# Where the last quarter of layer 0's gate projection runs, and where the last head group's prompt unit stands

## The chip, the core and the metric

The kernel runs on one core of one Trainium2 chip. A core has a matrix engine (TensorE, PE in the profile; its weight loads are shown as PEld), a vector engine (VectorE, DVE), an engine for activation functions (ScalarE, ACT), a general one (GpSimd, POOL) and a queue engine that issues transfers (SyncE, SP). The engines run at the same time, each through its own list of instructions in order, and wait for each other by semaphores. The metric is the time of one execution on the device, in microseconds (us); smaller is better. Of the kernel before, three runs took 864.18, 865.16 and 865.75 us, median 865.16.

## The reference, cut to what matters

One step of a two-layer network on 640 tokens: 512 latent ones ("sample") and 128 context ones ("prompt"), 1024 features each. Layer 0 is grouped-query attention with a gate, layer 1 a gated linear recurrence. The change is in layer 0, which per token stream computes:

```
shift, scale, gate = split(silu(cond) @ ada_w + ada_b)
h   = x * (1 + scale) + shift
q, k, v, g = split(h @ w_in)            # 1024, 256, 256, 1024 columns
q, k = rms_norm(q), rms_norm(k)         # with rotary positions on latent tokens
o   = softmax(q @ k.T / 8) @ v          # 16 query heads on 4 key heads of 64
out = (o * silu(g)) @ w_out
x   = layer_norm(alpha * x + gate * out)
```

Prompt tokens attend to prompt tokens only; sample tokens attend to 128 cached positions and all 512 sample tokens (640 keys). The part that the change moves is the last quarter of `silu(g)`: 256 of the 1024 gate columns, which are multiplied into the outputs of the last four query heads.

## The kernel before, in words

**Precision.** Matrices are kept as a high and a low part in a rounded fp32 format (`hi` and `lo`); a product takes three matmuls: hi by hi, hi by lo, lo by hi. The modulated input `h` is held feature by token in `hhi` and `hlo`, eight blocks (`KT`) of 128 features by 640 tokens. A weight arrives from memory as `raw` pieces of 512 KB; `split_piece` (line 217) casts the piece to `hi` on ScalarE and subtracts on VectorE for `lo`.

**The stream of raw pieces.** `order` (lines 357 to 374) lists all weight pieces in the order in which they are used, and `pump` (line 193) issues their transfers from SP's queue in this order, two ahead, into a ring of three buffers. So a piece cannot be issued before the one ahead of it in the list. `attn_w_in` is cut in chunks of 256 columns, two pieces each: chunks 0 to 3 are q, one per head group, and 6 to 9 are the gate. `ada_pieces(sup)` are eight pieces of the modulation's weights.

**Lead-in.** After keys and values, `lead_in` (line 658) computes q of head group 0 and then the gate: chunks 6 to 9, for each chunk two column blocks of 128 (`mt`) by two token halves of 320 (`j`), which is sixteen units. A unit is `feat_mms` (line 324), 24 matmuls into one PSUM bank, and a Silu on ScalarE into `gs` (line 746); `gs` has eight blocks of 128 columns by 640 tokens, and chunk `ch` and `mt` fill block `2 * (ch - 6) + mt`. Between the units stand the jobs that normalise, rotate, split and transpose q and k (`later`, with `settle` for the transposes). In the last `EARLY` = 2 units, attention is started by `next(att)`.

**Attention.** `att_gen` (line 885) runs over 36 units: for each of four head groups `c`, a `prompt_unit` and then eight `sample_unit`s (a head and a half of the sample queries each). A unit has fronts (scores, maximum, Exp with a sum; the reciprocal and the scaling on GpSimd follow), backs (transposes of the probabilities, copied out of PSUM) and an end. Fronts run two units ahead. Two neighbouring sample units share an end: `apply`, twenty TensorE instructions in the profile into `pot`, and `av_out` (line 786), which multiplies `gs` in place. `pot` and the prompt's `potp` share a pool with one buffer (`pop`). Blocks `2c` and `2c + 1` of `gs` belong to group `c`, and the prompt's `av_out` touches the last 128 tokens of both.

**PSUM.** In this phase there are two double banks (`bank2`, the scores), three single banks (`bank1`: q projection and transposes, ada, transposes of probabilities) and the one of `pop`. Each set is a ring that is handed out in the order in which the program is written.

**Side work.** `weave` (line 84) drives attention and, 0.62 times per step (`SIDE_B`), one step of a list called `side`, strictly in the list's order: `q1`, `q2`, `q3` (the q projections of groups 1 to 3, each with eight ada pieces), then `a` (the last ada), `w` (`prefetch_gen`: the first four pieces of the output projection's weights, in the room that the in-projection's weights leave) and `s` (`split_gs` of blocks 0 to 5). `split_gs` casts finished blocks of `gs` into `hhi` and subtracts into `hlo`, whose old contents, the modulated input, must no longer be needed. An item may have a condition: `q` of group `c` starts when fronts have come to group `c - 1`, `a` when a unit of group 3 has ended. `side.until(name)` forces a list item to its end at that point.

**The end of layer 0.** Blocks 6 and 7 are split last (line 1119), then come the other weight pieces, and from line 1260 on the output projection, token block by token block.

**Order.** All this lies in one block (`first_half`, lines 165 to 1121) whose instructions a planner lays out anew on each engine when the kernel is built; it may put an instruction that is ready ahead of one that was written earlier. Only what is marked `keep_in_program_order` stays in place. The program's order thus sets priorities and the rings of buffers, not the exact order on an engine.

Of the kernel before, what the change touches and what calls it, by code (L numbers as in the profile page):

```python
# [38 lines left out]
EARLY = 2  # L39
# [91 lines left out]
def hybrid_step(ctx: ExitStack, tc: tile.TileContext, a: dict, o: dict):  # L131
# [177 lines left out]
    def ada_gen(sups):  # L309
        for sup in sups:  # L310
            acc = rowp.tile([P, CW], F32, tag="row", name="acc")
            nc.gpsimd.dma_start(acc, a["ada_bias"][sup])
            for i in range(4):
                ps = bank1("adaps")
                ada_mms(ps, sup, i)
                nc.vector.tensor_tensor(acc, acc, ps[:, :CW], ALU.add)
                yield
            yield
            ada_out(sup, acc)
            yield  # L320
            if sup == 0:
                gate_load(0, nc.gpsimd)

    def feat_mms(ps, w, mt, j, hhi, hlo):
        c, t = slice(mt * P, (mt + 1) * P), slice(*HALVES[j])
        for k in range(KT):
            nc.tensor.matmul(ps[:, :320], w.hi(k)[:, c], hhi[:, k, t], start=(k == 0), stop=False)  # L327
            nc.tensor.matmul(ps[:, :320], w.hi(k)[:, c], hlo[:, k, t], start=False, stop=False)  # L328
            nc.tensor.matmul(ps[:, :320], w.lo(k)[:, c], hhi[:, k, t], start=False, stop=(k == KT - 1))  # L329

    def tok_gen(out, w, tt, hhi, hlo):
        t = slice(tt * P, (tt + 1) * P)
# [21 lines left out]
    def ada_pieces(sup):  # L354
        return [("ada_s", sup, k) for k in range(KT)]
# [7 lines left out]
        if c4 == 1:  # L363
            order.append(("rope",))
    FIRST = set(order)
    for c in (0, 6, 7, 8, 9):
        order.extend(pieces("attn_w_in", c))
    for c in range(3):
        order.extend(pieces("attn_w_in", c + 1))
        order.extend(ada_pieces(c))  # L370
    order.extend(ada_pieces(3))
    order.extend(("attn_w_out", nh, i) for nh, i in PIECES)
    order.extend(("rec_w_in", h, i) for h in range(RH) for i in range(5))
# [284 lines left out]
    def lead_in(att):  # L658
        backs = deque()
        ws = {0: first_w}  # L660

        def settle():
            while backs:
                backs.popleft()()

        rk = rtab.tile([P, NKV * TT], F32, name="rk")

        def k_stats():
            ss = rtab.tile([P, NKV * TT], F32, name="ssk")
            for tt0, m in UNITS:  # L670
                t = kr[tt0] = rtab.tile([P, m * CW], F32, tag=f"kr{tt0}", name="kr")
                for i in range(m):
                    nc.scalar.activation(t[:, i * CW:(i + 1) * CW], acc[tt0 + i][:, :CW], AF.Square)
                nc.vector.tensor_reduce(ss[:, NKV * tt0:NKV * (tt0 + m)], t[:].rearrange("p (h d) -> p h d", d=HD), AX.X, ALU.add)
            rsqrt(rk, ss, 1.0 / HD, NORM_EPS)

        def k_norm():
            for tt0, m in UNITS:
                for i in range(m):
                    tt = tt0 + i  # L680
                    nc.vector.tensor_tensor(view(kr[tt0], i * CW, [[HD, NKV], [1, HD]]),
                                            acc[tt][:, :CW].rearrange("p (h d) -> p h d", d=HD),
                                            view(rk, NKV * tt, [[1, NKV], [0, HD]]), ALU.mult)

        def k_rope(n):
            tt0, m = UNITS[n]
            rope_apply(kr[tt0], tt0, m, cosk, sink, kg, kr[tt0])
            if tt0 == TS:
                nc.gpsimd.dma_start(o["new_k"], kr[tt0])

        def k_split(n):
            tt0, m = UNITS[n]
            backs.append(split_k(kr[tt0], m, P * (tt0 + 1)))

        def v_job(tt):
            (nc.scalar.copy, nc.vector.tensor_copy)[tt % 2](vv[:, tt + 1, :], acc[tt][:, CW:])
            if tt == TS:
                nc.gpsimd.dma_start(o["new_v"], vv[:, tt + 1, :])

        rq = rtab.tile([P, NKV * TT], F32, name="rq")  # L700

        def q_stats():
            ss = rtab.tile([P, NKV * TT], F32, name="ssq")
            for n, (tt0, m) in enumerate(UNITS):
                squares(q0[n], m, ss[:, NKV * tt0:NKV * (tt0 + m)])
            rsqrt(rq, ss, 1.0 / HD, NORM_EPS)

        def q_job(n):
            tt0, m = UNITS[n]
            r = rope_apply(rms_apply(q0[n], m, rq, NKV * tt0), tt0, m, cosq, sinq, qg)  # L710
            back = q_split(r, tt0, m, 0, Xs[0], bank_any)
            backs.append(lambda: [back(i) for i in range(m)])

        ck = prep.tile([P, CW], F32, tag="ck", name="ck")
        tc.keep_in_program_order(nc.scalar.dma_start(ck, a["cache_k"]))
        tc.keep_in_program_order(nc.scalar.dma_start(vv[:, 0, :], a["cache_v"]))
        ws[6] = Weights("attn_w_in", 6, LEAD_LO)
        w = ws.pop(0)
        q0, kr = [], {}
        for n, (tt0, m) in enumerate(UNITS):  # L720
            ps = bank_any("pmm")
            for i in range(m):
                drain(tok_gen(ps[:, i * CW:(i + 1) * CW], w, tt0 + i, hhi, hlo))
            q0.append(ps)
            if n == 0:
                k_stats()
                for tt in range(TT):
                    v_job(tt)
                k_norm()
            else:  # L730
                k_rope(n - 1)
        open_rest()
        q_stats()
        k_rope(2)
        later = [lambda n=n: q_job(n) for n in range(3)] + [lambda: backs.append(split_k(ck, 1, 0))]
        later += [lambda n=n: k_split(n) for n in range(3)]
        step = 0
        for ch in range(6, 10):
            if ch < 9:
                ws[ch + 1] = Weights("attn_w_in", ch + 1, LEAD_LO)  # L740
            w = ws.pop(ch)
            for mt in range(2):
                for j, (t0, t1) in enumerate(HALVES):
                    ps = bank_any("gps")
                    feat_mms(ps, w, mt, j, hhi, hlo)
                    nc.scalar.activation(gs[:, 2 * (ch - 6) + mt, t0:t1], ps[:, :320], AF.Silu)
                    step += 1
                    if step % 2 or not later:
                        settle()
                    if step % 2 and later:  # L750
                        later.pop(0)()
                    if step > 16 - EARLY:
                        next(att)


# [129 lines left out]
    def att_gen(side):  # L885
        units = []
        for c in range(4):
            units.append(prompt_unit(c))
            units += [sample_unit(c, 2 * pr + j, qh) for pr in range(2) for qh in range(2) for j in range(2)]
        AHEAD = 2  # L890

        def fronts(u):
            if u >= len(units):
                return []
            c, fr = units[u][:2]
            front_of[0] = c
            side.until(f"q{c}")
            return list(fr)

        def run(f):  # L900
            f()
            tick()

        for u in range(AHEAD):
            for f in fronts(u):
                run(f)
                yield
        pending = []

        def flush():  # L910
            while pending:
                run(pending.pop(0))
                yield

        for u, (c, _, back, end) in enumerate(units):
            fr = fronts(u + AHEAD)
            for n, b in enumerate(back):
                run(b)
                yield
                if n == 1:  # L920
                    yield from flush()
                if n and fr:
                    run(fr.pop(0))
                    yield
            for f in fr:
                run(f)
                yield
            back_of[0] = c
            if end:
                pending.append(end if len(back) == 2 else end())  # L930
        yield from flush()
        while later:
            tick()
# [59 lines left out]
    def prefetch_gen():  # L993
# [2 lines left out]
        woa.append(ws.enter_context(pool("woa", 1)))  # L996
        yield from wo_gen(0, PIECES[:4], woa[0])

    def q_next(c):
        Xs[c] = xq[c % 2].tile([P, 4, NT], F32R, tag="X", name=f"X{c}")  # L1000
        yield from q_gen(c, Xs[c], ada_gen((c - 1,)))

    for c in range(1, 4):
        side.items.append((f"q{c}", q_next(c), lambda c=c: front_of[0] >= c - 1))
    side.items.append(("a", ada_gen((3,)), lambda: back_of[0] == 3))
    side.items += [("w", prefetch_gen()), ("s", split_gs(range(6)), lambda: back_of[0] == 3)]
    weave(att, side, SIDE_B)
# [634 lines left out]
```

## Time and profile before

The profile shows one execution, which took 863.82 us.

| quantity | value |
|---|---|
| median of three runs | 865.16 us |
| profiled execution | 863.82 us |
| its span, first to last instruction | 862.1 us |
| around the span | 1.7 us |
| instructions | 19366 |
| mean granted TensorE clock | 0.986 |
| moved by transfers | 92.50 MB |

The span falls into these stages: start, modulation, keys and values up to some 62 us; q of group 0 up to 73; the sixteen gate units from 72.9 to 135.6; attention with q projections beside it up to 281.7, where the last q matmul starts; the last head group up to 343.8; then the output projection and layer 1.

How to read the lines: a row of the view by stretch gives the stretch and its length, the busy time of each engine with its number of instructions, the granted TensorE clock (1.00 is full), the transfers' share and rate. A row of the timeline gives start, length, engine, line, operation, output and inputs with shapes and count; in square brackets the engine's idle time before it and what ended that. A row of the view of waits gives who waited for whom, total us, times, the longest. A row of groups ends with count, busy us, mean ns and the idle time before. The lines of the kernel are meant by L and a number.

### The profile page before, as it was taken

Reading aid. Unit: us, or ns where it says so; the run is one execution under the profiler, and the core shown is the slowest. Engines: PE = TensorE matmul, PEld = TensorE weight load, DVE = VectorE, ACT = ScalarE, POOL = GpSimd, SP = SyncE. Lnnn points to the kernel's source line nnn. Section 1 sums busy time; section 2 is a strip of 40 time slices with the busy share of each in tenths; the row PEclk is TensorE's granted clock in tenths of the full one; section 3 lists DMA queues with packets and bytes.
Section 4 is the critical chain, followed back from the end, with each engine's and each line's share of the span. In section 5 each row is a group of like instructions: output and inputs, shape, how many; then the busy total and the mean of one; then the engine's idle time right before and its main releaser. Section 6 shows DMA issues by size and latency. Waiting matters only on the chain.

```text
span 862.1 us, 19366 instructions
## 1 busy us (share of the span) xinstructions
PE 818.7 (95%) x8144; PEld 734.0 (85%) x8144; DVE 530.9 (62%) x952; ACT 384.0 (45%) x767; POOL 211.8 (25%) x263
## 2 busy tenths in 40 slices
PE   6999999989999998999999999999999999999993
PEld 4789998768778756888899999999999999897783
DVE  3556435755746656776437575757667576858384
ACT  2232536554655766232434544444444345443240
POOL 0123002434434652010001314142333233110101
PEclk9999999999999999999999999999999999999996
DMA  9932212143242162621223322332413323242221
GB/s 339 364 98 86 84 40 75 50 172 130 86 141 75 49 205 90 233 109 59 80 68 71 103 64 81 81 112 69 111 57 93 93 82 98 75 149 68 66 112 73
DMA packets 33990, 92.50 MB, mean 107 GB/s; under 512 B 5024, under 2 KB 12208, under 8 KB 33904
## 3 DMA queue, kind: packets, MB, share of 16 engines
q1 hardware_dynamic: 22992, 72.95, 25.0%
q0 software_dynamic: 4864, 14.44, 5.5%
q10 hardware_dynamic: 6048, 3.88, 1.5%
q8 instruction: 64, 1.05, 0.5%
q14 instruction: 22, 0.18, 0.1%
HBM read 82.06 MB, written 9.19 MB: 106 GB/s over the span
## 4 chain that ended last, share of the span: by engine, by line
PE 85%; DVE 6%; ACT 3%; DMA 2%; issue 2%; POOL 1%; ACTq 0%; DVEq 0%; POOLq 0%
PE rps L1192 7%; PE rps L1193 6%; PE rps L1194 6%; PE vgps L1182 4%; PE vgps L1184 4%; PE vgps L1183 4%; PE outp L1031 4%; PE pot L784 4%; PE outp L1032 4%; PE outp L1033 4%; PE pt L866 3%; PE lv L1324 2%; PE gps L327 2%; PE gps L328 2%; PE gps L329 2%; PE sc L757 2%
## 5 line engine op out<-in xcount | busy, mean ns | idle before, releaser
L1192 PE MATMUL rps<-h1hi,rhi 128*128 128x320 f32 x368 | 118.3, 321 | 0.0
L1193 PE MATMUL rps<-h1lo,rhi 128*128 128x320 f32 x368 | 113.7, 309 | 0.0
L1194 PE MATMUL rps<-h1hi,rlo 128*128 128x320 f32 x368 | 113.6, 309 | 0.0
L859 POOL TENSOR_SCALAR p<-p,rc 128x640 f32<-128x640 f32 x64 | 54.6, 856 | 69.2 <-DVE rc L858 53.0
L1192 PEld LDWEIGHTS rps<-h1hi,rhi 128*128 128x128 f32 x368 | 69.2, 188 | 1.3
L1193 PEld LDWEIGHTS rps<-h1lo,rhi 128*128 128x128 f32 x368 | 69.2, 188 | 0.0
L1194 PEld LDWEIGHTS rps<-h1hi,rlo 128*128 128x128 f32 x368 | 69.1, 188 | 0.0
L222 DVE TENSOR_TENSOR rlo<-raw,rhi 128x1024 fp32r<-128x1024 f32 x32 | 45.4, 1421 | 33.9 <-ACT rhi L221 33.9
L854 ACT ACTIVATE p<-sc,nm 128x640 f32<-128x640 f32 x64 | 51.2, 801 | 28.8 <-DVE nm L851 22.1
L1352 POOL COPY At<-near 32x160 f32<-32x160 f32 x32 | 14.0, 438 | 196.2 <-DVE near L1314 195.2
L851 DVE TENSOR_REDUCE nm<-sc 128x1 f32<-128x640 f32 x64 | 52.0, 819 | 15.5 <-PE sc L758 15.3
L1302 ACT COPY kc<-A 128x640 f32<-128x640 f32 x40 | 32.3, 807 | 59.4 <-DVE A L1333 51.7
L221 ACT CAST rhi<-raw 128x1024 fp32r<-128x1024 f32 x32 | 33.6, 1049 | 52.0 <-PE rps L1193 48.4
L866 PE MATMUL pt<-small,p 128*128 128x128 f32 x320 | 50.5, 279 | 2.5 <-ACT pts L762 1.3
L1182 PE MATMUL vgps<-rhi,h1hi 128*128 128x256 f32 x180 | 51.7, 287 | 1.2 <-ACT h1hi L982 1.2
L1184 PE MATMUL vgps<-rhi,h1lo 128*128 128x256 f32 x180 | 51.0, 283 | 0.4 <-DVE h1lo L983 0.4
L1183 PE MATMUL vgps<-rlo,h1hi 128*128 128x256 f32 x180 | 50.9, 283 | 0.0
L762 ACT COPY pts<-pt 128x512 f32<-128x512 f32 x64 | 36.3, 590 | 29.4 <-PE pt L866 29.2
L866 PEld LDWEIGHTS pt<-small,p 128*128 128x128 f32 x320 | 37.4, 141 | 11.3 <-issue 7.4
L757 PE MATMUL sc<-kk,X 128*128 128x320 f32 x128 | 43.0, 344 | 2.9 <-ACT p L854 2.7
L1182 PE MATMUL vgps<-wspare,h1hi 128*128 128x256 f32 x140 | 41.7, 298 | 0.0
L327 PE MATMUL gps<-hhi,whi 128*128 128x320 f32 x128 | 40.0, 312 | 0.4 <-ACT X L610 0.4
(291 smaller groups left out, 2393.5 us busy)
## 6 DMA issues: line engine op xcount, KB each, us to landing
raw<-in_rec_w_in SPq DMA_DIRECT2D x40, 512.0 KB, 3.6
raw<-in_ada_s SPq DMA_DIRECT2D x32, 512.0 KB, 3.6
raw<-in_ada_m SPq DMA_DIRECT2D x16, 512.0 KB, 8.4
raw<-in_attn_w_in SPq DMA_DIRECT2D x16, 512.0 KB, 4.2
raw<-in_attn_w_out SPq DMA_DIRECT2D x8, 512.0 KB, 4.0
raw<-in_rec_w_out SPq DMA_DIRECT2D x8, 512.0 KB, 3.8
x1d<-y SPq DMA_DIRECT2D x5, 512.0 KB, 2.6
rx<-x1d POOLq DMA_DIRECT2D x20, 128.0 KB, 3.2
```

Of the source, the lines that this page charges most:

```text
L327: nc.tensor.matmul(ps[:, :320], w.hi(k)[:, c], hhi[:, k, t], start=(k == 0), stop=False)
L757: nc.tensor.matmul(out, X[:, h, t0:t0 + P], kk[:, c, k0:k1], start=True, stop=False)
L851: nc.vector.tensor_reduce(nm[:, 0:1], sc[:, :, :320], AX.XY, ALU.max, negate=True)
L854: nc.scalar.activation(halves(p[:]), sc[:, :, :320], AF.Exp, bias=nm[:, 0:1], accum_out=su[:, 0:1])
L859: nc.gpsimd.tensor_scalar(p, p, rs[:, 0:1], 1.0, ALU.mult, ALU.mult)
L866: nc.tensor.transpose(pt[:, i * 256 + q * P:i * 256 + (q + 1) * P], ps[q][:, (k0 + i) * P:(k0 + i + 1) * P], ident)
L1182: nc.tensor.matmul(out, h1hi[:, k, t], hi, start=(k == 0), stop=False)
L1183: nc.tensor.matmul(out, h1hi[:, k, t], lo, start=False, stop=False)
L1184: nc.tensor.matmul(out, h1lo[:, k, t], hi, start=False, stop=(k == KT - 1))
L1192: nc.tensor.matmul(ps[:, j, :320], hi[:, k, :], h1hi[:, k, t], start=(k == 0), stop=False)
L1193: nc.tensor.matmul(ps[:, j, :320], hi[:, k, :], h1lo[:, k, t], start=False, stop=False)
L1194: nc.tensor.matmul(ps[:, j, :320], lo[:, k, :], h1hi[:, k, t], start=False, stop=(k == KT - 1))
```

## The change

The reordered and moved parts are these; nothing that is computed changes.

- In the stream of raw pieces, chunk 9 goes from behind chunk 8 to behind the pieces of group 3's q and of the third ada.
- `feat_mms` becomes the generator `feat_gen` with the same 24 matmuls and a stop after each twelve.
- `lead_in` runs chunks 6 to 8, twelve units. `settle` comes after every unit, a job of `later` after two of three.
- `gate_gen(9, mt)` computes chunk 9 as two side items, `g0` and `g1`, which stand behind `q3` and ahead of `a`, and may start when fronts have come to group 3. Its weights are split as in `q_gen`, on ScalarE and VectorE. Each takes its banks from the three single ones, and has two units with a Silu each.
- In group 3 the prompt unit comes behind the eight sample units.
- Ahead of the ends of group 3's units, `side.until` forces `g0` (first two pairs) or `g1` (the other pairs and the prompt unit).

```diff
-    def feat_mms(ps, w, mt, j, hhi, hlo):
+    def feat_gen(ps, w, mt, j, hhi, hlo):
         c, t = slice(mt * P, (mt + 1) * P), slice(*HALVES[j])
         for k in range(KT):
...
             nc.tensor.matmul(ps[:, :320], w.lo(k)[:, c], hhi[:, k, t], start=False, stop=(k == KT - 1))
+            if k % 4 == 3:
+                yield
...
-    for c in (0, 6, 7, 8, 9):
+    for c in (0, 6, 7, 8):
         order.extend(pieces("attn_w_in", c))
     for c in range(3):
         order.extend(pieces("attn_w_in", c + 1))
         order.extend(ada_pieces(c))
+    order.extend(pieces("attn_w_in", 9))
     order.extend(ada_pieces(3))
...
-        for ch in range(6, 10):
-            if ch < 9:
+        for ch in range(6, 9):
+            if ch < 8:
                 ws[ch + 1] = Weights("attn_w_in", ch + 1, LEAD_LO)
...
-                    feat_mms(ps, w, mt, j, hhi, hlo)
+                    drain(feat_gen(ps, w, mt, j, hhi, hlo))
                     nc.scalar.activation(gs[:, 2 * (ch - 6) + mt, t0:t1], ps[:, :320], AF.Silu)
                     step += 1
-                    if step % 2 or not later:
-                        settle()
-                    if step % 2 and later:
+                    settle()
+                    if step % 3 and later:
                         later.pop(0)()
-                    if step > 16 - EARLY:
+                    if step > 12 - EARLY:
                         next(att)
...
-            units.append(prompt_unit(c))
-            units += [sample_unit(c, 2 * pr + j, qh) for pr in range(2) for qh in range(2) for j in range(2)]
+            pairs = [sample_unit(c, 2 * pr + j, qh) for pr in range(2) for qh in range(2) for j in range(2)]
+            units += pairs + [prompt_unit(c)] if c == 3 else [prompt_unit(c)] + pairs
...
             back_of[0] = c
+            if c == 3 and end:
+                side.until("g0" if u < len(units) - 5 else "g1")
             if end:
                 pending.append(end if len(back) == 2 else end())
...
+    w9 = []
+
+    def gate_gen(ch, mt):
+        if not w9:
+            w9.append(Weights("attn_w_in", ch, (nc.vector, nc.vector)))
+            yield
+        for j, (t0, t1) in enumerate(HALVES):
+            ps = bank1("gps")
+            yield from feat_gen(ps, w9[0], mt, j, hhi, hlo)
+            nc.scalar.activation(gs[:, 2 * (ch - 6) + mt, t0:t1], ps[:, :320], AF.Silu)
+            yield
...
     for c in range(1, 4):
         side.items.append((f"q{c}", q_next(c), lambda c=c: front_of[0] >= c - 1))
+    side.items += [(f"g{mt}", gate_gen(9, mt), lambda: front_of[0] == 3) for mt in range(2)]
     side.items.append(("a", ada_gen((3,)), lambda: back_of[0] == 3))
     side.items += [("w", prefetch_gen()), ("s", split_gs(range(6)), lambda: back_of[0] == 3)]
```

## The prediction

> **What bounds the kernel now.** I read the page from the top: engine shares, then the chain that ended last.
>
> ```profile
> PE 818.7 (95%) x8144; PEld 734.0 (85%) x8144; DVE 530.9 (62%) x952; ACT 384.0 (45%) x767; POOL 211.8 (25%) x263
> ...
> PE 85%; DVE 6%; ACT 3%; DMA 2%; issue 2%; POOL 1%; ACTq 0%; DVEq 0%; POOLq 0%
> ```
>
> TensorE is busy 95% of the span and holds 85% of the chain. Moving matmuls from one place to another therefore changes nothing by itself; only TensorE's idle time can be won or lost. So the next view was busy time by stretch, in this order: lead-in gate matmuls, attention with the q projections beside it, then the end of attention cut at three places, the last group as a whole, and five microseconds of it.
>
> ```profile
> core 0: us, PE busy (x) PEld busy (x) DVE busy (x) ACT busy (x) POOL busy (x), PEclk, DMA share, GB/s
> 72.90:131.30 58.40, 58.01 (x419) 57.84 (x418) 26.51 (x42) 22.30 (x39) 4.10 (x2) 1.00 0.20 66
> 120.90:281.65 160.75, 154.35 (x1282) 130.04 (x1281) 93.39 (x207) 90.14 (x197) 58.09 (x62) 0.99 0.29 101
> 281.65:296.60 14.95, 13.90 (x121) 10.75 (x121) 10.79 (x27) 11.48 (x26) 11.81 (x12) 1.00 0.19 71
> 296.60:312.00 15.40, 14.81 (x125) 10.28 (x122) 8.36 (x20) 9.46 (x25) 5.99 (x7) 1.00 0.28 98
> 312.00:343.80 31.80, 27.02 (x221) 18.96 (x220) 19.91 (x41) 21.26 (x42) 11.42 (x16) 1.00 0.47 153
> 281.65:343.80 62.15, 55.73 (x463) 39.99 (x461) 39.06 (x87) 42.19 (x93) 29.22 (x34) 1.00 0.35 120
> 325.00:330.00 5.00, 2.94 (x21) 2.24 (x20) 5.00 (x8) 4.56 (x9) 0.79 (x1) 1.00 0.66 207
> ```
>
> The lead-in is full (0.39 idle in 58.40). Attention with a q projection beside it is idle 6.40 of 160.75, 4.0%. The last stretch, from the last q matmul at 281.65 to the output projection, is idle 62.15 - 55.73 = 6.42, or 10.3%, and most of that lies late: 1.05, 0.59, then 4.78. The last group lacks matmuls that wait for nothing, and that is the whole prize: 6.4 us. Who is waited for there:
>
> ```profile
> PE sc L757 <- ACT p L854: 1.5, 2, 0.8
> PE adaps L265 <- DMA raw<-in_ada_s: 1.3, 1, 1.3
> PE pt L866 <- ACT pts L762: 1.3, 1, 1.3
> ```
>
> ScalarE leads (1.5 + 1.3). This matters, because the change brings ScalarE work there.
>
> **The change part by part.** *Gate units.* Four of the sixteen units (24 matmuls of 320 columns and a Silu each) leave the lead-in. Their pace:
>
> ```profile
> 76.63 0.44 ACT L746 ACTIVATE gs<-gps 128x320 f32<-128x320 f32 x1 [2.19 <-PE gps L329]
> 80.15 0.44 ACT L746 ACTIVATE gs<-gps 128x320 f32<-128x320 f32 x1 [3.08 <-PE gps L329]
> ```
>
> One unit each 3.52, so the lead-in loses 4 x 3.52 = 14.1 and the last group gains 14.1 of matmuls: zero together, before idle time.
>
> *Holes.* If the last group with gates is as dense as attention with q matmuls (4.0% idle), 76.25 us hold 3.05 idle instead of 6.42: -3.4. Bounds: nothing (0), and all holes (-6.4). I take -3.4 because this is the same head-group work with the same kind of filler beside it. The share is reached only if the ada matmuls of line 265, which come after the gates in the side list, slide later into the 4.78.
>
> *Table loads.* Silu and Exp do not share a table. The place where the two already alternate, at the end of the lead-in:
>
> ```profile
> 135.61 1.28 ACT L746 ACT_TABLE_LOAD   x1
> 136.90 0.44 ACT L746 ACTIVATE gs<-gps 128x320 f32<-128x320 f32 x1
> ...
> 138.08 1.28 ACT L854 ACT_TABLE_LOAD   x1
> ```
>
> and TensorE at the same time:
>
> ```profile
> 138.11 0.65 PE L784 MATMUL potp<-pts,vv 128*64 128x256 f32 x4 [0.73 <-ACT pts L762]
> ```
>
> A Silu among Exps costs two loads of 1.28 and its own 0.44, 3.0 us in which no softmax step runs. A unit takes 3.5 us of TensorE even if nothing is put between, and the sixteen sample Exps of the group alone come every 4.8 us of the 76, so I count four separate Silus, eight loads, 10.3 us of ScalarE. ScalarE's work in the stage grows from 42.2 of 62.15 to 42.2 + 10.3 + 4 x 0.44 + two weight casts of 1.05 = 56.4 of 76.25: 74%, against 56% (90.14 of 160.75) beside the q matmuls. On the path, one such Silu cost TensorE 0.73 above, with matmuls beside it as here. Bounds per Silu: 0 (all under gate matmuls) and 3.0 (all on the chain). I take the row: 4 x 0.73 = +2.9, bounds 0 to +12.0.
>
> The Trainium skill, "ScalarE: Activation LUTs" (What ACT_TABLE_LOAD costs), puts a switch at about 2.66 us, a load of 1283 ns plus a drain of about 1380 ns, and advises batching calls by table set, which this change does the opposite of. The trace agrees on the load, but shows no drain: the load from 135.61 ends at 136.89 and Silu starts at 136.90. By the page's switch this term would be 2.66 / 1.28 times as large, +6.0 (an estimate), and the whole sum +5.4; I go by the row.
>
> *Weights of the last quarter.* Their two pieces take the place of the next two ada pieces in SP's order, so they are issued where these are now:
>
> ```profile
> 290.78 0.80 SPq L208 DMA_DIRECT2D raw<-in_ada_s  x2
> ```
>
> with the time to landing, and the splits of a weight pair in the lead-in:
>
> ```profile
> raw<-in_ada_s SPq DMA_DIRECT2D x2, 512.0 KB, 3.6
> ```
>
> ```profile
> L222 DVE TENSOR_TENSOR wlo<-raw,whi 128x1024 fp32r<-128x1024 f32 x8 | 10.0, 1252 | 4.7 <-ACT whi L221 4.7
> L221 ACT CAST whi<-raw 128x1024 fp32r<-128x1024 f32 x8 | 8.4, 1050 | 4.1 <-PE gps L328 3.1 <-PE pmm L336 0.8
> ```
>
> Landing near 294.4, cast 1.05, low part 1.25, the second piece a microsecond behind: usable at 296.7 and 297.8. The first gate unit is emitted after the q side is done, whose last transposes are the last of these rows:
>
> ```profile
> 180.10 0.53 PE L608 MATMUL qps<-identr,qs 128*128 128x128 f32 x4 [0.57 <-DVE pts L762]
> ...
> 185.94 0.50 PE L608 MATMUL qps<-identr,qs 128*128 128x128 f32 x4 [1.99 <-DVE qs L601]
> ...
> 293.72 0.53 PE L608 MATMUL qps<-identr,qs 128*128 128x128 f32 x4 [0.24 <-ACT pts L762]
> ```
>
> So it is late by some 3 us while it holds one of the three single PSUM banks through which the probability transposes (line 863) rotate. Nearest rows: the first two, stalls around the second q group's late weights, 0.57 and 1.99. I take the smaller, +0.6 (0 to +2.0), because scores and two banks go on. The ada pieces queued behind on SP move by two splits, and their matmuls come after the gates anyway: nothing, with 1.3 (the wait row) if that cover is gone.
>
> *Splits that must wait.* `split_gs` overwrites hhi and hlo, which the gates now still read. Today these run as soon as q3 ends:
>
> ```profile
> L983 POOL TENSOR_TENSOR hlo<-gs,hhi 128x640 fp32r<-128x640 f32 x6 | 9.3, 1556 | 2.0 <-PE qmm L336 1.8 <-ACT hhi L982 0.2
> L982 ACT CAST hhi<-gs 128x640 fp32r<-128x640 f32 x6 | 4.2, 723 | 1.7 <-PE qmm L335 1.7
> ```
>
> That is 4.2 of ScalarE and 9.3 of GpSimd, pushed behind the gates to where GpSimd scales the probabilities (line 859) and the weight splits for the output projection sit. What crowding does there is the 325 to 330 row: VectorE 5.00, ScalarE 4.56 of 5, TensorE idle 2.06, of which one wait for ScalarE's copies (in the waits above) is 1.3. I add one such wait: +1.3 (0 to +2.5).
>
> *Prompt unit last.* Its four pscp reductions and Exps leave the start of the group and its apply follows the last pair, in the one-buffer pool of `pot`. Today's end:
>
> ```profile
> 340.94 2.38 PE L784 MATMUL pot<-pts,vv 128*64 128x256 f32 x20 [0.52 <-DVE pts L762]
> 343.84 0.50 PE L1031 MATMUL outp<-wohi,hhi 128*128 128x512 f32 x1 [0.53 <-DVE gs L789]
> 344.18 0.39 PE L1032 MATMUL outp<-wolo,hhi 128*128 128x512 f32 x1
> 344.40 0.39 PE L1033 MATMUL outp<-wohi,hlo 128*128 128x512 f32 x1
> ```
>
> and VectorE's:
>
> ```profile
> 343.36 0.42 DVE L789 TENSOR_TENSOR gs<-pot,gs 128x256 f32<-128x256 f32 x1 [2.48 <-PE pot L784]
> ...
> 346.84 0.82 DVE L983 TENSOR_TENSOR hlo<-gs,hhi 128x640 fp32r<-128x640 f32 x1
> ```
>
> Matmuls, multiply, output projection: 0.53 idle. Then it is matmuls, multiply, potp, multiply, output projection: a second 0.53, +0.5. Its transposes could as well fill the 0.52 ahead of the last pair, and rows 6 and 7 of gs both wait for it, one more low part (0.82) ahead of the projection's k = 6: bounds -0.5 to +1.4. Today's single low part ended 3.8 after the projection began, and the six rows ahead of it keep TensorE busy for 18 matmuls at 0.22, 4.0, so I leave the term at 0.5.
>
> *Lead-in squeezed.* The q, k and rope jobs now follow each other in 12 units instead of 16. VectorE has 26.5 of 58.4 there, so the work fits. TensorE's idle 0.39 in this stretch I let double: +0.4, bounds 0 and one unit, +3.5.
>
> Sum: -14.1 + 14.1 - 3.4 + 2.9 + 0.6 + 1.3 + 0.5 + 0.4 = **+2.3**. The profiled execution took 863.82 (span 862.1 and 1.7 around it), which would become 866.1. The three runs' median of 865.16 is 1.3 above it; the forecast is for a median, 865.16 + 2.3 = **867.5**.
>
> **The rivals.** *ScalarE's loads hide, and it gets faster.* Place: from 296.6 to the end of attention. Gate matmuls queue behind each other while the tables are swapped, and ada's matmuls move into the late holes: 0.59 + 4.78 = -5.4, weights and loads 0, crowding, tail and lead-in as above (+2.2): -3.2, **862.0**. For it speaks that ScalarE stays under 75%; against it, that two of the three waits shown are already ScalarE's. It holds from the point where one Silu costs TensorE less than (3.2 - 1.7) / 4 = 0.37. Chance 0.28.
>
> *They cancel*: holes -5.4, four Silus at 0.73 and the +2.2 come to -0.3: **864.9**. Chance 0.20.
>
> *The gates do not reach the holes.* The kernel's planner pulls work that is ready ahead, as it did with the casts of line 982; then they are used up beside the second to last pairs. Only 0.59 is filled: 2.3 + 2.8 = +5.1, **870.3**. Chance 0.10.
>
> *Every swap is on the chain*: 12.0 in place of 2.9, +11.4, **876.6**; with half of that, 872. For it, softmax cannot run without Exp; against it, two score banks and two probability units are in flight. Chance 0.10.
>
> **How the numbers follow.** My forecast, slower by 1.8 to 4, has 0.32 (its own range 866.9 to 869.5). A measurement here tells 0.2%, 1.7 us, from no change. Slower: 0.32 + 0.10 + 0.10 = 0.52; same 0.20; faster 0.28. Range 861 to 873: it leaves out a fuller filling of the holes below, about 0.07, and the worse part of the swaps above, about 0.07.
>
> **What would show it.** Right: Silus of the gate generator between Exps with up to eight new table loads; TensorE idle after them on pts or p; gate matmuls from about 282 on (14 earlier than 296.7); idle of the last group between 6 and 9 in some 76 us; two multiplies of line 789 in series at the end. Wrong: fewer than four new loads, idle of the last group under 4, a lead-in that loses less than 13 us, or output-projection weights that come late.

## The result, and the profile after

The changed kernel takes 870.46 us (median of 15 runs, 867.54 to 876.65); the kernel before took 865.21 beside it (15 runs). The ratio is 1.0066, 95% interval 1.0052 to 1.0081: slower, by 5.3 us between the medians. The forecast was 867.5.

The profiled execution of the changed kernel took 867.54, the fastest of its runs, so spans tell less than stages. The view by stretch, cut at the first gate matmul, the first q matmul beside attention, the last q matmul, the first matmul of the output projection and layer 1's first q matmul, shows the kernel before:

```profile
72.92:139.26 66.34, 65.22 (x474) 64.01 (x472) 30.26 (x47) 29.96 (x54) 5.12 (x3) 1.00 0.20 63
139.26:281.65 142.39, 136.72 (x1151) 113.45 (x1148) 87.08 (x196) 80.17 (x178) 57.05 (x61) 0.99 0.31 108
281.65:343.84 62.19, 55.73 (x463) 39.99 (x461) 39.06 (x87) 42.23 (x93) 29.22 (x34) 1.00 0.35 119
343.84:420.61 76.77, 75.12 (x400) 63.97 (x401) 49.06 (x89) 23.39 (x40) 5.66 (x10) 1.00 0.31 113
420.61:862.05 441.44, 422.73 (x5098) 399.03 (x5096) 287.81 (x458) 186.35 (x373) 101.78 (x140) 0.98 0.29 88
```

and the changed one with the same cuts, with two more rows for the lead-in's gap and the time behind it (columns: stretch and length, then PE, PEld, DVE, ACT, POOL busy with counts, granted clock, transfers' share and GB/s):

```profile
72.87:132.32 59.45, 53.32 (x387) 51.82 (x385) 28.93 (x50) 25.56 (x51) 5.99 (x5) 0.97 0.17 57
132.32:275.03 142.71, 135.46 (x1144) 112.78 (x1141) 86.85 (x193) 77.16 (x172) 54.49 (x59) 0.99 0.32 106
275.03:349.21 74.18, 69.69 (x560) 54.45 (x558) 40.38 (x88) 56.32 (x108) 32.00 (x34) 1.00 0.35 115
349.21:426.03 76.82, 75.17 (x401) 63.96 (x401) 49.80 (x90) 24.02 (x41) 5.67 (x10) 1.00 0.33 113
426.03:865.77 439.74, 420.87 (x5097) 397.67 (x5096) 287.76 (x458) 186.18 (x373) 101.97 (x140) 0.98 0.29 88
80.10:84.34 4.24, 0.00 (x0) 0.00 (x0) 3.42 (x6) 1.05 (x2) 0.03 (x1) 0.96 0.00 0
84.34:88.00 3.66, 3.66 (x20) 3.66 (x21) 2.90 (x5) 1.69 (x3) 0.00 (x0) 0.58 0.00 0
```

Up to the output projection the change costs 349.21 - 343.84 = 5.4, the same as the medians say. It is made of two stages. The last group grew by 12.0, not by the 14.1 of the gate matmuls that came in: it won 2.1, its idle time fell from 6.46 to 4.49. The lead-in fell by 6.9, not by the 14.1 that went out: it lost 7.2. TensorE's idle time there rose from 1.12 to 6.13, and one gap makes most of it, with half a clock behind it. (Layer 1 was 1.7 shorter here; the last experiment shows that this goes by the execution.)

The waits of TensorE in the changed lead-in, and the queue at that place:

```profile
PE qps L611 <- DVE qs L604: 4.3, 1, 4.3
PE sc L759 <- ACT pp L816: 1.9, 1, 1.9
```

```profile
84.34 1.26 PE L611 MATMUL qps<-identr,qs 128*128 128x128 f32 x8 [4.28 <-DVE qs L604]
85.40 0.59 PE L327 MATMUL gps<-hhi,whi 128*128 128x320 f32 x1
85.79 0.47 PE L328 MATMUL gps<-hlo,whi 128*128 128x320 f32 x1
```

With a transposition after every unit, the first q transposes (`qps`) stand behind the second gate unit. Their data come from VectorE, which does the jobs that normalise, rotate and split q:

```profile
77.46 0.69 DVE L570 TENSOR_TENSOR kr<-kr,u 128x512 f32<-128x512 f32 x1
80.17 0.69 DVE L527 TENSOR_TENSOR qn<-pmm,rq 128x512 f32<-128x512 f32 x1 [2.01 <-POOL rq L187]
...
83.60 0.69 DVE L604 TENSOR_TENSOR qs<-r,qs 128x512 fp32r<-128x512 f32 x1 [0.68 <-ACT qs L603]
```

The first q job cannot begin before 80.17, because the reciprocal root comes from GpSimd then, and the job takes four microseconds. The transposes were due at 80.1. TensorE goes through its list in order, so ten gate units stood behind one wait; the first of them began at 85.40, right behind the transposes and without a wait of its own. The transposes are the same as before; what costs the time is their place in the queue.

### The profile page after: what moved, and what is told of

It is laid out like the page before. It is cut to its first block, busy times and chain, and to the rows that moved or that the text cites. A ratio compares the mean times of both kernels' runs of the same rounds, so it can differ in the third digit from the quotient of the medians.

```text
span 865.8 us, 19376 instructions
## 1 busy us (share of the span) xinstructions
PE 817.7 (94%) x8144; PEld 734.2 (85%) x8144; DVE 531.3 (61%) x952; ACT 391.1 (45%) x773; POOL 213.1 (25%) x263
## 4 chain that ended last, share of the span: by engine, by line
PE 80%; DVE 8%; ACT 5%; issue 2%; POOL 2%; DMA 2%; SPq 0%; ACTq 0%; DVEq 0%; POOLq 0%
PE rps L1209 7%; PE rps L1210 6%; PE rps L1211 6%; PE vgps L1199 4%; PE vgps L1201 4%; PE vgps L1200 4%; PE outp L1048 4%; PE outp L1049 3%; PE pot L786 3%; PE outp L1050 3%; PE pt L868 3%; PE lv L1341 2%; PE sc L759 2%; PE gps L327 2%; PE gps L329 2%
```

## The experiments

Times are medians, each beside runs of the kernel before on the same chip (865.3 in the first four, 865.0 in the next four, 864.7 in the last).

**The new pace alone, with sixteen units.** The pace is the two lines that place the jobs of q and k and their transposes between the gate units. On the kernel before:

```diff
-                    if step % 2 or not later:
-                        settle()
-                    if step % 2 and later:
+                    settle()
+                    if step % 3 and later:
                         later.pop(0)()
```

> The kernel before with sixteen gate units in the lead-in, but with the new pace of the jobs beside them (transposes emitted after every unit, a job after two of three). Theory A, the new pace: the first q transposes are queued behind the second gate unit, ahead of their data, so TensorE waits 4.3 us near 80 us and runs its next microseconds at half clock; 4.5 to 5.5 us over the kernel before (865.2), so 869.7 to 870.7. Rival B, twelve units are simply too few to cover the chain of q and k jobs: with sixteen the wait is gone, within 1 us of before.

869.24, ratio 1.0056 (1.0043 to 1.0069). The wait of 4.3 is there, with the slow clock behind it:

```profile
81.40:85.70 4.30, 0.06 (x1) 0.06 (x1) 3.48 (x6) 1.05 (x2) 0.03 (x1) 0.74 0.00 0
85.70:89.40 3.70, 3.70 (x18) 3.70 (x19) 2.95 (x5) 1.69 (x3) 0.00 (x0) 0.50 0.00 0
```

The pace alone costs 4.0 us by medians, 0.5 short of what theory A asked. The wait does not come from the number of units: for it, rival B falls.

**The transposes held back by a job**, on the changed kernel:

```diff
-        def settle():
-            while backs:
+        def settle(left=0):
+            while len(backs) > left:
                 backs.popleft()()
...
-                    settle()
+                    settle(1 if step < 9 else 0)
```

> The changed kernel, with one job's transposes always held back by one more job until the ninth unit; still twelve units. Theory A: the 4.3 us wait and the slow clock after it go, 4.5 to 5.5 us under the changed kernel (870.5): 865.0 to 866.0. Rival B: the chain is what is too long, the wait moves to a later transposition or to the start of attention; 869 or more. Rival C, the table loads cost most of the loss: 869 or more too, with the lead-in's idle time gone and the last group's unchanged.

866.07, ratio 1.0012 (1.0002 to 1.0023): 4.4 under the changed kernel, at the edge of what theory A asked. Lead-in 55.52, which is 3.9 less; last group 74.36, unchanged:

```profile
74.43:129.95 55.52, 53.27 (x386) 51.04 (x384) 29.91 (x54) 26.20 (x53) 6.74 (x6) 0.98 0.19 61
129.95:273.15 143.20, 135.88 (x1144) 112.92 (x1141) 85.93 (x189) 76.04 (x168) 53.77 (x58) 0.99 0.30 106
273.15:347.51 74.36, 69.83 (x560) 54.39 (x558) 40.78 (x88) 56.24 (x108) 31.05 (x34) 1.00 0.34 114
```

The lead-in is still 3.3 above 66.34 - 14.1 = 52.2. The other wait of the list, 1.9 at the start of attention, is still there. Behind it the granted clock fell to 0.50 in this profile, from 128 to 130, which it did not do in the changed kernel; by the clock from 127 to the end of the lead-in that is 1.4 us of the 3.3 (an estimate).

**No table swaps beside the last group.** On the changed kernel, in `gate_gen`; the last 256 gate columns stay without their Silu:

```diff
-            nc.scalar.activation(gs[:, 2 * (ch - 6) + mt, t0:t1], ps[:, :320], AF.Silu)
+            nc.scalar.activation(gs[:, 2 * (ch - 6) + mt, t0:t1], ps[:, :320], AF.Copy)
```

> The changed kernel with a Copy in place of the four Silus that lie beside the last head group (the last 256 gate columns stay without their Silu): no table swaps there, the lead-in as in the changed kernel. Theory A: the loads cost only what ScalarE is waited for in the last group, 1.5 to 3 us: 867.5 to 869. Rival C: they cost 4 us or more: 866.5 or less.

867.43, 3.0 under the changed kernel. In the last group:

```profile
277.35:349.30 71.95, 69.61 (x559) 54.38 (x558) 40.74 (x88) 46.21 (x100) 31.07 (x34) 1.00 0.35 118
```

2.2 shorter, idle 2.34 in place of 4.49, ScalarE 10.1 less busy. The swaps are real, and the smaller of the two large costs: the medians lie at the edge of theory A's range and short of rival C's.

**The prompt unit last, alone**, on the kernel before:

```diff
-            units.append(prompt_unit(c))
-            units += [sample_unit(c, 2 * pr + j, qh) for pr in range(2) for qh in range(2) for j in range(2)]
+            pairs = [sample_unit(c, 2 * pr + j, qh) for pr in range(2) for qh in range(2) for j in range(2)]
+            units += pairs + [prompt_unit(c)] if c == 3 else [prompt_unit(c)] + pairs
```

> The kernel before with nothing but the prompt unit of the last head group moved behind the eight sample units. By the prediction's term for the end of attention: +0.5 us (865.7), bounds -0.5 to +1.4, with two multiplies of the gate in series at the end. Rival D: its latency at the end is worth more than the term, 2 us or more (867.2 or more).

862.34, ratio 0.998 (0.9963 to 0.9997): faster, against the term and against rival D. Yet the last group is only 0.2 shorter (61.97). So it was run once more:

> The kernel before with only the prompt unit of the last group moved, once more. It was 2.9 us under before by medians, but only 0.2 us shorter in the last group. If the gain is real: 862 to 863.5, ratio below 1, and a last group shorter by 1 us or more, or a later stage that is shorter again. If it was the spread of the runs: within 1 us of before.

862.54, ratio 0.9984 (0.9967 to 1.0), last group 61.42, 0.8 shorter:

```profile
282.45:343.87 61.42, 54.47 (x464) 39.98 (x462) 39.31 (x86) 41.30 (x92) 31.07 (x34) 1.00 0.36 121
```

The direction held twice, 2.9 and 2.4 us by medians. The stages show less than a third of it.

**The prompt unit first again**, in the changed kernel:

```diff
-            units += pairs + [prompt_unit(c)] if c == 3 else [prompt_unit(c)] + pairs
+            units += [prompt_unit(c)] + pairs
...
-                side.until("g0" if u < len(units) - 5 else "g1")
+                side.until("g1")
```

> The changed kernel with the prompt unit first in the last group as in the kernel before; all four gate units are then forced ahead of its end. If the order of the prompt unit is worth the 2.9 us of the fourth run here too: 873. If it is worth the 0.2 us that the stage showed: 870 to 871. A rival: less, since with the prompt unit first the end of attention has only one multiply in series: 869.5 to 870.

871.92, 1.5 above the changed kernel; the last group 75.94 against 74.18, although two gate units here share a pair of swaps (three round trips, six loads). Part of the 1.5 can be the lead-in, which had more slow clock in this profile (61.55). The rival, less with one multiply in series, falls: behind the pairs the prompt unit is worth about 1.8 in this stage. The edit also forces all four gate units ahead of the group's first end; what that does by itself was not run.

**Silu from Exp, so that no table is swapped**, on the kernel with the held-back transposes:

```diff
-            nc.scalar.activation(gs[:, 2 * (ch - 6) + mt, t0:t1], ps[:, :320], AF.Silu)
+            g = gs[:, 2 * (ch - 6) + mt, t0:t1]
+            nc.scalar.activation(g, ps[:, :320], AF.Exp, scale=-1.0)
+            nc.vector.tensor_scalar(g, g, 1.0, 1.0, ALU.add, ALU.mult)
+            nc.vector.reciprocal(g, g)
+            nc.vector.tensor_tensor(g, ps[:, :320], g, ALU.mult)
```

> The changed kernel with the held-back transposes of the second run, and the four late Silus made from Exp on ScalarE and three operations on VectorE, so that no table is swapped beside the last head group. If wait and swaps simply add: 866.1 less the 3.0 that the Copy saved, 863.1, about 2 us under the kernel before (865.3); the last group 72 us from its last q matmul to the output projection. Rival: the three VectorE operations (some 1.3 us a unit, a bank held longer) take back what the swaps cost: 865 or more.

869.73: the rival, and more than it asked. The last group took 79.88. VectorE's groups there show the work that came in:

```profile
L1015 DVE RECIPROCAL gs<-gs 128x320 f32<-128x320 f32 x4 | 8.6, 2143 | 0.0
...
L1014 DVE TENSOR_SCALAR gs<-gs 128x320 f32<-128x320 f32 x4 | 2.1, 517 | 0.9 <-ACT gs L1013 0.9
L1016 DVE TENSOR_TENSOR gs<-gps,gs 128x320 f32<-128x320 f32 x4 | 1.9, 477 | 0.0
```

A full-width reciprocal takes 2.14 us where the operations beside it take 0.5; I had counted 1.3 us for all three and it is 3.1. TensorE's longest wait in the stage is a different one, for a piece of ada's weights:

```profile
PE adaps L265 <- DMA raw<-in_ada_s: 3.2, 1, 3.2
```

Behind it the granted clock was 0.57 from 331 to 335. That the reciprocals cause this wait, because the last gate unit holds its bank until 319.8 and ada's matmuls and transfers follow late, is argued and was not run.

**The jobs one unit earlier**, on the kernel just shown:

```diff
-                    if step % 3 and later:
+                    if step % 4 and later:
```

> The same with the jobs one unit earlier (a job after three of four units), so that the last keys are transposed a unit before attention starts. Theory: the 1.9 us wait for the first Exps at the start of attention falls back to the 0.7 of the kernel before, 1 us under the run beside it: 862. Rival: the earlier jobs meet their data late, as in the changed kernel, and a wait of 1 us or more at the third or fourth unit takes it back: 863 or more.

865.48, 4.3 under the run beside it. The time was not reached, as its last group was still 78.49, and the number is the rival's. But the rival's wait is not there, and the lead-in was what the experiment asked, and more: 52.59.

**Both pace settings with the change's own Silus**, so the last two diffs of the lead-in and no other:

> The changed kernel with nothing mended but the lead-in: transposes held back by one job and a job after three of four units, the four late Silus as in the change. Lead-in to the first q matmul 52.6 us as in the run with the Exps, last group 74.2 as in the changed kernel: 13.8 less and 12.0 more than the kernel before, so 863.2 (1.8 under 865.0), all eight swaps included. Rival: what the lead-in wins, the q stage gives back (144.8 against 142.4 with the Exps): 865 or more.

864.15, ratio 0.9998 (0.9982 to 1.0015).

```profile
74.33:126.92 52.59, 51.39 (x378) 49.99 (x376) 27.72 (x45) 26.07 (x48) 5.14 (x3) 1.00 0.18 60
126.92:269.90 142.98, 135.36 (x1151) 112.48 (x1148) 87.30 (x197) 79.01 (x176) 55.57 (x60) 1.00 0.31 107
269.90:344.41 74.51, 69.85 (x559) 54.38 (x557) 40.59 (x88) 56.28 (x108) 31.04 (x34) 1.00 0.35 114
```

The lead-in's 14.1 is there almost whole (13.8), with 1.20 idle. With two mended settings of the pace, what the change lost is gone: 6.3 us under the changed kernel, level with the one before. The median lies between the theory's 863.2 and the rival's 865. In this profile the q stage gives nothing back, but its clock was full there; in the other three kernels with this lead-in the q stage took 143.8 to 144.8, each with some microseconds at half clock. So the rival is not wholly out.

**The same with a Tanh**, whose missing half goes into the multiply by the gate in group 3:

```diff
-            nc.scalar.activation(gs[:, 2 * (ch - 6) + mt, t0:t1], ps[:, :320], AF.Silu)
+            g = gs[:, 2 * (ch - 6) + mt, t0:t1]
+            nc.scalar.activation(g, ps[:, :320], AF.Tanh, scale=0.5)
+            nc.vector.scalar_tensor_tensor(g, g, 1.0, ps[:, :320], ALU.add, ALU.mult)
...
+            defer(D_OUTS, lambda: tc.keep_in_program_order(nc.vector.scalar_tensor_tensor(gt, tv, 0.5, gt, ALU.mult, ALU.mult)))
```

> The same lead-in, and the four late Silus made from a Tanh (half the input, one operation on VectorE, the remaining factor of a half in the multiply by the gate). Theory: by the page on activation functions in the Trainium skill Tanh lies in the set of Exp, so no table is loaded beside the last group and one VectorE operation a unit of 0.5 us is hidden; last group 72 us as with the Copy, 861 to 862. Rival: VectorE's operation holds the bank as the three of the Exp version did, last group 76 or more: 866 or more. If Tanh is not in the set, eight loads stay and it is at least 863.

863.14, ratio 0.9986 (0.9968 to 1.0004). No table was loaded beside the last group; ScalarE there was 46.1 busy, as with the Copy, but the stage was 73.88, nearer to the 74.51 with the Silus than to the Copy's 72.24 below. The 861 to 862 was missed by one.

**The same with a Copy**, which again leaves out the Silu of the last 256 gate columns:

> The same lead-in with a Copy for the four late Silus (256 gate columns without their Silu): the bound for any version without swaps. Last group 72 us, 2.2 under the run with the swaps beside it: 861. If the swaps are worth the 3.0 us of the medians of the third run: 860.2. If 863 or more, the swaps cost nothing once the lead-in is mended.

859.81, ratio 0.9954 (0.9938 to 0.9971); last group 72.24. The swaps are worth 2.3 by the stage (74.51 less 72.24) and 4.3 by the medians (864.15 less 859.81); where the other 2.0 lie is open.

**The kernel before, a second profile.**

> The kernel before once more, for a second profile of it. In its first profile the part from layer 1's first q matmuls to the end took 441.4 us, in the profiles with only the prompt unit moved 439.1 to 439.2. If that part belongs to the kernel: 441 again. If it goes by the execution: anything from 439 to 441.5, with lead-in, q stage and last group at 66.35, 142.4 and 62.2 again; then the 2.5 to 3 us that moving the prompt unit wins by medians are not explained by one pair of profiles.

863.20; lead-in 66.35, q stage 143.1, last group 62.26, and 439.0 from layer 1's first q matmul on, where the first profile had 441.4. That part goes by the execution, the lead-in and the last group repeat to 0.1. So the 2.4 to 2.9 us of the prompt unit's order are not explained by layer 1, and only 0.2 to 0.8 of them by its own stage: that stays open. The clock may have a part: of the first 12 runs with the prompt unit last, the eight with a mean granted clock of 0.990 or more took 860.1 to 862.6 us and the other four 864.5 to 867.6, while 23 of the 28 runs of the kernel before beside them had 0.986 to 0.988.

| kernel | lead-in | q stage | last group | median |
|---|---|---|---|---|
| before | 66.3 | 142.4 | 62.2 | 865.2 |
| changed | 59.4 | 142.7 | 74.2 | 870.5 |
| pace alone, sixteen units | 72.3 | 141.0 | 64.0 | 869.2 |
| changed, transposes held back | 55.5 | 143.2 | 74.4 | 866.1 |
| changed, Copy for Silu | 59.7 | 143.0 | 72.0 | 867.4 |
| prompt unit last alone | 66.3 | 142.5 | 62.0 | 862.3 |
| changed, prompt unit first | 61.5 | 141.6 | 75.9 | 871.9 |
| held back, Silu from Exp | 55.6 | 143.2 | 79.9 | 869.7 |
| both pace settings, Silu from Exp | 52.6 | 144.8 | 78.5 | 865.5 |
| both pace settings | 52.6 | 143.0 | 74.5 | 864.2 |
| both pace settings, Tanh | 52.6 | 144.6 | 73.9 | 863.1 |
| both pace settings, Copy | 52.6 | 143.8 | 72.2 | 859.8 |

Of the kernels that compute the reference, the one with nothing but the prompt unit moved is the fastest: below the kernel before in both of its comparisons, though in the second only to the edge of the interval. The Tanh version lies 1.5 under before, with an interval that still holds 1.

## Why the prediction was right, and where it was not

The direction was right, and the time lies in the range of 861 to 873, though above the 866.9 to 869.5 that the forecast gave for its own sum. But the sum of +2.3 was made for the wrong reason: its parts in the last group came to +1.9 and measured -2.1, its part in the lead-in was +0.4 and measured +7.2. That the two misses together still gave the forecast sign is luck. Two of the prediction's own signs tell it: the lead-in lost 6.9, where less than 13 was to mean wrong, and the last group was idle 4.49, where 6 to 9 was to mean right.

*Lead-in squeezed* is the step that failed: +7.2 is above its own upper bound of +3.5. It argued from VectorE's share, 26.5 of 58.4, that the work fits. It does: the same jobs fit into 52.6 with both pace settings mended. What counted was not the share but when one result is there, against where its reader stands in TensorE's queue. The rows to read were VectorE's of the kernel before:

```profile
80.21 0.69 DVE L524 TENSOR_TENSOR qn<-pmm,rq 128x512 f32<-128x512 f32 x1 [2.01 <-POOL rq L187]
...
84.64 0.69 DVE L601 TENSOR_TENSOR qs<-r,qs 128x512 fp32r<-128x512 f32 x1 [1.69 <-ACT qs L600]
```

The first q job could not begin before 80.2. Its transposes were written behind the third unit and ran behind the fourth, at 87; the change writes them behind the second, and there, at 80.1, they were due. The 7.2 are 4.3 of wait; 1.5 of clock (42% of 3.66 us); and 1.1 more idle at the start of attention. There the transposes of the last keys were written a unit ahead of attention's first step and are now written right at it, so the prompt's scores come after the last unit and nothing lies beside the first Exps (1.9 waited, against 0.7; with the jobs one unit earlier it is 0.7 again). A wait of 0.4 at 88.17 in the kernel before is gone, so 0.7 is not placed; part of it can be the cut, as 387 TensorE instructions lie ahead of it here and 378 with both pace settings.

*Holes* were put at -3.4. With the Copy, which has no swaps, the last group takes in 14.1 and grows from 62.0 (prompt unit last, no gates; 61.4 in its second profile) to 71.95: 4.1 (3.6) filled. The mechanism was right, and the size too, as far as it can be told from late weights and crowding. The stretches of the changed kernel show where:

```profile
289.70:305.00 15.30, 15.30 (x113) 14.75 (x110) 5.83 (x12) 11.27 (x17) 3.17 (x4) 1.00 0.00 1
305.00:316.00 11.00, 10.62 (x80) 9.21 (x78) 1.94 (x5) 9.43 (x16) 6.49 (x6) 1.00 0.01 1
316.00:349.20 33.20, 29.91 (x256) 20.15 (x256) 20.02 (x43) 24.88 (x53) 17.20 (x19) 1.00 0.59 191
```

TensorE is full while the gates run, and ada's matmuls did slide later: the late stretch is idle 3.29, where it was 4.78.

*Table loads* at +2.9: eight, as counted, in four separate round trips (a load ahead of the Silu, another ahead of the next Exp).

```profile
L1012 ACT ACT_TABLE_LOAD x4 | 5.1, 1283 | 0.1
L856 ACT ACT_TABLE_LOAD x4 | 5.1, 1283 | 0.5 <-DVE nm L853 0.4
```

Taken away they give 2.2 to 2.3 by the stage, 3.0 and 4.3 by medians, so the term was of the right size. What the count missed: the two loads of the lead-in's own round trip are gone, since its last Silu now ends before the first Exp, so the net is six (eleven against five). The waits show how they cost:

```profile
PE adaps L265 <- ACT gs L1012: 1.5, 1, 1.5
PE sc L759 <- ACT p L856: 1.5, 2, 0.8
PE potp L786 <- DVE gs L791: 0.6, 1, 0.6
PE outp L1048 <- DVE gs L791: 0.5, 1, 0.5
```

The longest single wait was not of a softmax step but for the last Silu: it ran at 318.16, after casts, Exps and two loads, and ada's matmuls waited for the gate's bank until then. The Trainium skill, "ScalarE: Activation LUTs" (What ACT_TABLE_LOAD costs), makes a switch 2.66 us with its drain; the trace agrees on the load of 1283 ns alone, here again with the Silu 0.02 us behind it (from 307.07 to 308.35, Silu at 308.37). That the sum by this switch, +5.4, lies beside the measured +5.3 is luck: its term of +6.0 is not what the swaps were worth.

```profile
307.07 1.28 ACT L1012 ACT_TABLE_LOAD   x1
308.37 0.44 ACT L1012 ACTIVATE gs<-gps 128x320 f32<-128x320 f32 x1
...
318.16 0.44 ACT L1012 ACTIVATE gs<-gps 128x320 f32<-128x320 f32 x1
```

*Prompt unit last* at +0.5: the second multiply in series is in the list above, 0.6 for `potp` and 0.5 for the projection, as said. But the order as a whole is worth between -0.2 and -0.8 on the kernel before and -1.8 in the changed one, where the forcing of the gate units moved with it. The sign of the term was wrong: it priced the end alone. What the unit costs at its old place, ahead of the group, was not priced, and these runs show only the difference, not which of its steps make it.

*Late weights* (+0.6) and *crowding* (+1.3) cannot be seen apart. The first gate matmul ran at 291.81, not from 282 on; 7.2 of that is the lead-in's. TensorE was full over the first gate units, and no wait in the list goes back to the splits of hhi and hlo or to GpSimd; together with the holes they are within the 4.1. As terms of their own they look too dear.

Of the rivals, the one that the forecast called a gain, loads that hide, would have needed 0.37 per Silu; it was 0.55 by the stage (2.2 / 4). Gates that miss the holes did not come about, although that rival's 870.3 lies beside the measured 870.5, and neither did swaps that all stand on the chain.

## What to carry to other kernels

Before moving work out of a full stretch, look up for each job that was hidden beside it when its input arrives, and where its reader stands in the queue of the bound engine; a share of busy time does not answer this. When a stage gets shorter, give each result a unit of its own between producer and reader: here a lag of one job and jobs one unit earlier were worth 6.3 us of 870. A change in two stages is best priced and run by stage, because a gain in one can be hidden by a loss in the other.

## What was not expected of the hardware

One wait of 4.3 us cost 1.5 more: the granted clock was 0.58 in the 3.66 us after it, 0.50 in the run with the pace alone, and 128x320 matmuls took 0.47 in place of 0.31. All four profiles with this wait show the fall. Shorter waits can bring it too, and the kernel before showed it already: behind the wait of 1.99 at 185.94, one of the prediction's rows, the granted clock was 0.50 from 187 to 189, and four transposes took nearly twice what they took ahead of it:

```profile
171.39 0.60 PE L866 MATMUL pt<-small,p 128*128 128x128 f32 x4
...
188.14 1.12 PE L866 MATMUL pt<-small,p 128*128 128x128 f32 x4
```

Behind the wait of 1.85 at the start of attention the clock fell in three profiles (transposes held back, the same with Silu from Exp, prompt unit first) and stayed full in two (the changed kernel and its Copy). The Trainium skill, "TensorE: Matmul & The Clock Gate" (What's actually happening), has the clock at half after an idle window of about 3.4 us. The wait of 4.3 agrees with that; the falls behind 1.85 and 1.99 show that here less can be enough, in some executions. The prediction priced its waits without the clock, and for the long one the clock belongs into the price. The reciprocal of 128x320 took 2143 ns on VectorE, 4.5 times the multiply beside it. Four Tanhs among the Exps of the last group needed no table load, where four Silus needed eight.
